# Feed-forwards with the gate and up weights as the stationary operand

## The chip, the cores and the metric

The kernel runs on one core of one Trainium2 chip. The metric is device time in microseconds for one execution, as the median of several runs. TensorE does the matrix products, VectorE and ScalarE the elementwise work, GpSimd (POOL) a few small steps; SyncE (SP) issues the transfers that bring the weights from HBM.

## What is computed

Three layers of a small model for 256 tokens with 1024 features, everything in float32. A first block (attention and gated convolution, modulated by rows computed from `c`) is followed by two more: gated linear attention, then differential attention. Each of the three ends in a gated feed-forward of 2816 hidden columns. The reference, cut to what the change concerns:

```python
def swiglu(h, w_gate, w_up, w_down):
    return (jax.nn.silu(h @ w_gate) * (h @ w_up)) @ w_down

# first block: one layer
x  = layer_norm(DEEPNORM_ALPHA * x + g1[:, None, :] * mix, ln1_g[l], ln1_b[l])
ff = swiglu(modulate(x, sh2, sc2), w_gate[l], w_up[l], w_down[l])
x  = layer_norm(DEEPNORM_ALPHA * x + g2[:, None, :] * ff, ln2_g[l], ln2_b[l])

# second block: two layers
def swiglu_2(h, w_in, w_out):
    g, u = split_cols(h @ w_in, [D_FF_2, D_FF_2])
    return (jax.nn.silu(g) * u) @ w_out

h = h + mix
h = h + swiglu_2(rms_norm(h, norm_ffn[i]), ffn_w_in[i], ffn_w_out[i])
gate = jax.nn.sigmoid(rms_norm(h, ple_norm[i]) @ ple_w_gate[i])
h = h + gate * (p[i] @ ple_w_proj[i])
```

## The kernel before

**Tiles.** The 256 tokens are two token tiles of 128, `x[0]` and `x[1]`, with tokens on the partitions and 1024 features along the free dimension. A product over the features needs them on the partitions, so each token tile is transposed on TensorE in blocks of 128x128 (`tr`, line 124, against the identity) and evacuated into tiles `xh` and `xl` of the class `XT` (L164). Every operand is split into two parts whose sum is the float32 value, `h` (a cast) and `l` (the rest, a subtraction). A product then is three matmuls: h by h, h by l, l by h (`mm3`, L157: lines L159, L160, L162). Of an `XT`, tile `[t][n]` holds four of the eight feature blocks for one token tile.

**Weights.** They are streamed once. `stage` (L127) issues the transfers, `gran` (L141) splits a granule of 128x1024 into `wh` (ScalarE's cast, L150) and `wl` (VectorE's subtraction, L151). Staging has eight buffers, the split weights five.

**The feed-forward** (`ffn`, L684) runs over eleven chunks of 256 hidden columns; there are three feed-forwards, so 33 chunks. Of a chunk, each granule holds two feature blocks by 512 columns: 256 of gate, 256 of up. The stationary operand of a matmul is a block of tokens (128 features x 128 tokens), the moving one 512 weight columns, and the result `ps[t]` holds tokens on the partitions, gate in the first 256 columns, up in the others: 8 feature blocks x 2 token tiles x 3 parts = 48 matmuls of 512 columns. ScalarE takes Silu of the gate half (L714, or L717 with the token's factor as `scale`), VectorE multiplies by the up half (L715, L718). The product `sg` has tokens on the partitions, and the down projection needs hidden columns there, so four transposes (L720, recorded at L124) put it into a PSUM bank, from which `hh` and `hl` are split (L723, L724). The down projection of the chunk before, 24 matmuls of 512 columns into four accumulating banks, stands behind the gate and up matmuls of the present one. The last two chunks are multiplied at the end, a token tile and a bank at a time (`finish`, L232).

**The factor r.** The second and third feed-forward (in `tail_layer`) stand behind an RMS norm whose factor per token, `rs[t]`, is one number per partition and is applied after the matmuls, to gate and up. `rms_of` (L741) computes it beside the first chunk. In the first feed-forward there is no such factor (`rs` is None); its input comes from `norm_pair` (L655), which normalizes token tile 0, then token tile 1: a residual and its sums (L662, L663), a mean and variance, the normalization (L674), transposes, an affine step per block (L191), a cast (L177) and a subtraction (L178). In the other two, `residual_rms` (L733) adds the residual (L736), transposes and evacuates with a gain (`put_gain`, L184 and L185).

**Order.** A scheduler sets the order on each engine from the program's order, dependences and buffers; it interleaves the transposes of a token tile with matmuls that are ready. PSUM has eight banks, four for `mm()` and four for `ac()`; the four accumulators of the down projection are the latter, so gate/up products and the transposed product share four.

The columns of the granule, as the gate/up matmuls read them:

```python
wh, wl = gran(stage(gu(g, c)), (2, 512))
for t in range(2):
    for i in range(2):
        kb = g * 2 + i
        xh, xl = xt(kb, t)
        mm3([ps[t]], xh, xl, [wh[:, i]], [wl[:, i]], kb == 0, kb == KB - 1)
```

## Time and profile before

| what | value |
|---|---|
| median of 3 runs | 1100.68 us (1100.53 to 1101.87) |
| span of the profiled execution | 1096.2 us |
| TensorE matmuls busy | 1028.7 us (94%), 4770 instructions |
| TensorE weight loads busy | 819.9 us (75%) |
| VectorE busy | 669.1 us (61%) |
| ScalarE busy | 569.7 us (52%) |
| HBM read | 192.60 MB, 177 GB/s over the span |

The span is the time between the first and last recorded instruction of one profiled execution; the runs are timed without the profiler. PE stands for TensorE's matmuls (transposes among them), PEld for its weight loads, DVE for VectorE, ACT for ScalarE. Matmuls are pipelined, so their recorded lengths overlap, and what a matmul takes in a stream is the distance from its start to the next one's. PEclk is the granted clock, 1.00 or 0.50 (2.4 or 1.2 GHz) of TensorE.

### The profile page before, as it was taken

Reading aid. Unit: us, or ns where it says so; the run is one execution under the profiler, and the core shown is the slowest. Engines: PE = TensorE matmul, PEld = TensorE weight load, DVE = VectorE, ACT = ScalarE, POOL = GpSimd, SP = SyncE. Lnnn points to the kernel's source line nnn. Section 1 sums busy time; section 2 is a strip of 40 time slices with the busy share of each in tenths; the row PEclk is TensorE's granted clock in tenths of the full one; section 3 lists DMA queues with packets and bytes.
Section 4 is the critical chain, followed back from the end, with each engine's and each line's share of the span. In section 5 each row is a group of like instructions: output and inputs, shape, how many; then the busy total and the mean of one; then the engine's idle time right before and its main releaser. Section 6 shows DMA issues by size and latency. Waiting matters only on the chain.

```text
span 1096.2 us, 13449 instructions
## 1 busy us (share of the span) xinstructions
PE 1028.7 (94%) x4770; PEld 819.9 (75%) x4770; DVE 669.1 (61%) x1037; ACT 569.7 (52%) x910; POOL 105.4 (10%) x76
## 2 busy tenths in 40 slices
PE   2888998899999989999999999998998999999998
PEld 1664767678888867888788888886776778888886
DVE  3775568645555654764755556577877675545644
ACT  2354546645545466654644445466656464444543
POOL 0011150302200040000000000004011000000000
PEclk9888899899999999999999999999999999999999
DMA  8864558467866606444665667543442366666711
GB/s 281 283 224 154 191 202 298 145 210 231 258 189 193 206 12 187 160 133 155 192 190 178 190 192 234 170 154 118 154 141 92 95 193 191 184 186 189 240 66 39
DMA packets 130864, 194.53 MB, mean 177 GB/s; under 512 B 10447, under 2 KB 92867, under 8 KB 130797
## 3 DMA queue, kind: packets, MB, share of 16 engines
q1 hardware_dynamic: 130584, 193.48, 55.8%
q8 instruction: 37, 0.61, 0.2%
q10 hardware_dynamic: 212, 0.20, 0.1%
q14 instruction: 31, 0.25, 0.1%
HBM read 192.60 MB, written 1.05 MB: 177 GB/s over the span
## 4 chain that ended last, share of the span: by engine, by line
PE 78%; DVE 10%; ACT 4%; DMA 2%; POOL 2%; issue 2%; SPq 1%; DVEq 0%; ACTq 0%; POOLq 0%
PE mmb L162 16%; PE mmb L160 15%; PE mmb L159 15%; PE acb L159 7%; PE acb L160 7%; PE acb L162 7%; PE acb L124 2%; POOL rs L265 2%; PE mmb L124 2%; DVE wl L151 2%; DMA st<-in_w_ada_dram 1%; ACT wh L150 1%; DVE part L333 1%; DVE xl L178 1%; PE acb L1054 1%
## 5 line engine op out<-in xcount | busy, mean ns | idle before, releaser
L151 DVE TENSOR_TENSOR wl<-st,wh 128x1024 fp32r<-128x1024 f32 (+4 forms) x292 | 357.2, 1228 | 243.6 <-ACT wh L150 240.1
L150 ACT CAST wh<-st 128x1024 fp32r<-128x1024 f32 (+4 forms) x292 | 301.3, 1038 | 262.0 <-PE mmb L162 162.4
L159 PE MATMUL mmb<-wh,xh 128*128 128x512 f32 (+4 forms) x904 | 358.8, 399 | 6.8 <-ACT wh L150 3.5
L162 PE MATMUL mmb<-wh,xl 128*128 128x512 f32 (+4 forms) x904 | 352.0, 394 | 7.3 <-DVE xl L178 7.0
L160 PE MATMUL mmb<-wl,xh 128*128 128x512 f32 (+4 forms) x904 | 355.4, 394 | 0.9 <-DVE wl L151 0.7
L162 PEld LDWEIGHTS mmb<-wh,xl 128*128 128x128 f32 x904 | 173.0, 191 | 45.6 <-DVE xl L178 9.4
L159 PEld LDWEIGHTS mmb<-wh,xh 128*128 128x128 f32 x904 | 172.8, 192 | 43.2 <-ACT xh L177 4.3
L160 PEld LDWEIGHTS mmb<-wl,xh 128*128 128x128 f32 x904 | 173.5, 192 | 35.5 <-DVE wl L151 3.0
L160 PE MATMUL acb<-wl,hh 128*128 128x512 f32 x216 | 85.3, 395 | 0.0
L159 PE MATMUL acb<-wh,hh 128*128 128x512 f32 x216 | 84.8, 393 | 0.0
L162 PE MATMUL acb<-wh,hl 128*128 128x512 f32 x216 | 67.2, 392 | 0.0
L747 POOL TENSOR_TENSOR rsx<-rsx,mhalf 128x1 f32<-128x1 f32 x12 | 10.3, 856 | 460.1 <-DVE rsx L746 460.1
L265 POOL TENSOR_TENSOR rs<-rs,mhalf 128x8 f32<-128x8 f32 (+1 forms) x18 | 32.7, 1820 | 207.7 <-DVE rs L264 175.1
L159 PEld LDWEIGHTS acb<-wh,hh 128*128 128x128 f32 x216 | 40.5, 188 | 10.3 <-ACT wh L150 0.8
L160 PEld LDWEIGHTS acb<-wl,hh 128*128 128x128 f32 x216 | 40.6, 188 | 9.1 <-issue 0.5
L162 PEld LDWEIGHTS acb<-wh,hl 128*128 128x128 f32 x216 | 40.6, 188 | 8.6
L338 POOL TENSOR_TENSOR part<-st,part 128x512 f32<-128x512 f32 x21 | 32.1, 1530 | 7.5 <-issue 6.0
L717 ACT ACTIVATE sg<-mmb,rsx 128x256 f32<-128x256 f32 x44 | 20.8, 474 | 22.9 <-PE mmb L162 20.8
L151 DVE TENSOR_TENSOR wxl<-st,wxh 128x1024 fp32r<-128x1024 f32 x22 | 26.8, 1221 | 5.2 <-ACT wxh L150 5.0
L150 ACT CAST wxh<-st 128x1024 fp32r<-128x1024 f32 x22 | 22.7, 1050 | 9.7 <-DMA st<-in_ffn_w_out_dram 4.8
L718 DVE SCALAR_TENSOR_TENSOR sg<-mmb,rsx,sg 128x256 f32<-128x256 f32 x44 | 20.9, 480 | 10.8 <-ACT sg L717 10.8
L184 ACT ACTIVATE xh<-acb,cols 128x128 fp32r<-128x128 f32 x64 | 20.7, 367 | 8.9 <-PE acb L124 6.1
(307 smaller groups left out, 1110.0 us busy)
## 6 DMA issues: line engine op xcount, KB each, us to landing
st<-in_ffn_w_in_dram SPq DMA_DIRECT2D x176, 256.0 KB
st<-in_ffn_w_out_dram SPq DMA_DIRECT2D x44, 512.0 KB
st<-in_w_ada_dram SPq DMA_DIRECT2D x32, 512.0 KB
st<-in_diff_w_in_dram SPq DMA_DIRECT2D x24, 512.0 KB
st<-in_w_gate_dram SPq DMA_DIRECT2D x44, 256.0 KB
st<-in_w_up_dram SPq DMA_DIRECT2D x44, 256.0 KB
st<-in_w_down_dram SPq DMA_DIRECT2D x22, 512.0 KB
st<-in_w_ada_dram SPq DMA_DIRECT2D x32, 256.0 KB
```

What stands on the lines that cost most here:

```text
L124: T.transpose(o, i, ident)
L150: A.copy(h[:, :n], src)
L151: V.tensor_sub(l[:, :n], src, h[:, :n].bitcast(F32))
L159: T.matmul(p_, xh, wh, start=start, stop=False)
L160: T.matmul(p_, xh, wl, start=False, stop=False)
L162: T.matmul(p_, xl, wh, start=False, stop=stop)
L178: V.tensor_sub(l, v, h.bitcast(F32))
L184: A.activation(h[:, i, :], b, AF.Copy, scale=g)
L265: G.tensor_tensor(r[:, :n], r[:, :n], mhalf[:, :n], op=OP.pow)
L338: G.tensor_add(part, w(kb), bias if kb == 0 else part)
L717: A.activation(sg, ps[t][:, 0:256], AF.Silu, scale=rs[t])
L718: V.scalar_tensor_tensor(sg, ps[t][:, 256:512], rs[t], sg, op0=OP.mult, op1=OP.mult)
```

## The change

In the feed-forwards the operands of the gate and up matmuls change places. The stationary operand is now a block of the weights (128 features x 128 hidden columns), the moving one a feature block of all 256 tokens (`xt.tokens(kb)`). The result has hidden columns on the partitions and tokens along the free dimension, as the down projection wants it; `ps[0]` holds the gate product of two column blocks, `ps[1]` the up product. A chunk has 8 feature blocks x 4 column blocks x 3 parts = 96 matmuls of 256 columns instead of 48 of 512. The four transposes of the product and its PSUM bank go; Silu, the product, `hh` and `hl` are each one operation on 512 columns, from `sg` in SBUF.

The token's factor r now runs along the free dimension. `across` spreads it: two diagonal matrices (identity times r), two matmuls with a matrix of ones into a PSUM bank, a copy to `rw`. Gate is multiplied by `rw` on VectorE before Silu; the factor of up is applied to the output of the down projection, in `residual_rms`. The `XT` tiles hold both token tiles (three tiles of twice the size for six). Other products read the same blocks as before.

```diff
-    xtp = ctx.enter_context(tc.tile_pool(name="xtp", bufs=6))
+    xtp = ctx.enter_context(tc.tile_pool(name="xtp", bufs=3))
...
-            self.h[t][n] = xtp.tile([P, 4, P], F32R, name="xh", tag="xh")
-            self.l[t][n] = xtp.tile([P, 4, P], F32R, name="xl", tag="xl")
...
+                self.h[n] = xtp.tile([P, 4, S], F32R, name="xh", tag="xh")
+                self.l[n] = xtp.tile([P, 4, S], F32R, name="xl", tag="xl")
...
+        def tokens(self, kb):
+            n, i = divmod(kb, 4)
+            return self.h[n][:, i, :], self.l[n][:, i, :]
...
+        def across(r):
+            rb = mm()
+            for t in range(2):
+                dg = sm.tile([P, P], F32, name="dg", tag="dg", bufs=2)
+                V.tensor_scalar(dg, ident, r[t], None, op0=OP.mult)
+                T.matmul(rb[:, t * P:(t + 1) * P], onesP, dg, start=t == 0, stop=t == 1)
+            rw = wk.tile([P, S], F32, name="rw", bufs=1)
+            A.copy(rw, rb[:, 0:S])
+            return rw
...
-                for t in range(2):
-                    for i in range(2):
-                        kb = g * 2 + i
-                        xh, xl = xt(kb, t)
-                        mm3([ps[t]], xh, xl, [wh[:, i]], [wl[:, i]], kb == 0, kb == KB - 1)
+                for i in range(2):
+                    kb = g * 2 + i
+                    xh, xl = xt.tokens(kb)
+                    for u in range(2):
+                        for j in range(2):
+                            o = ps[u][:, j * S:(j + 1) * S]
+                            ws = slice(u * 256 + j * P, u * 256 + j * P + P)
+                            T.matmul(o, wh[:, i, ws], xh, start=kb == 0 and j == 0, stop=False)
+                            T.matmul(o, wl[:, i, ws], xh, start=False, stop=False)
+                            T.matmul(o, wh[:, i, ws], xl, start=False, stop=kb == KB - 1 and j == 1)
+            if c == 0 and rs is not None:
+                rw = across(rs)
...
-            tp = mm()
-            tv = tp.rearrange("p (a b) -> p a b", b=S)
-            for t in range(2):
-                sg = wk.tile([P, 256], F32, name="sg", tag="sg", bufs=3)
-                if rs is None:
-                    A.activation(sg, ps[t][:, 0:256], AF.Silu)
-                    V.tensor_mul(sg, ps[t][:, 256:512], sg)
-                else:
-                    A.activation(sg, ps[t][:, 0:256], AF.Silu, scale=rs[t])
-                    V.scalar_tensor_tensor(sg, ps[t][:, 256:512], rs[t], sg, op0=OP.mult, op1=OP.mult)
-                for i in range(2):
-                    tr(tv[:, i, t * P:(t + 1) * P], sg[:, i * P:(i + 1) * P])
+            sg = wk.tile([P, 2, S], F32, name="sg", tag="sg", bufs=2)
+            gv, uv = v3(ps[0], S), v3(ps[1], S)
+            if rw is None:
+                A.activation(sg, gv, AF.Silu)
+            else:
+                V.tensor_tensor(sg, gv, rw[:, None, :].to_broadcast([P, 2, S]), op=OP.mult)
+                A.activation(sg, sg, AF.Silu)
+            V.tensor_mul(sg, uv, sg)
...
-            A.copy(hh, tv)
-            V.tensor_sub(hl, tv, hh.bitcast(F32))
+            A.copy(hh, sg)
+            V.tensor_sub(hl, sg, hh.bitcast(F32))
...
-            V.tensor_add(x[t][:, hs], src[t][n], x[t][:, hs])
+            if r is None:
+                V.tensor_add(x[t][:, hs], src[t][n], x[t][:, hs])
+            else:
+                V.scalar_tensor_tensor(x[t][:, hs], src[t][n], r[t], x[t][:, hs], op0=OP.mult, op1=OP.add)
```

Three places show what moves. On TensorE, at the start of the first feed-forward, the order before is this (`acb` is a PSUM bank that takes transposes of `x0` or `x1`, `mmb` a product, `ident` the identity; the transposes of `x0` stand further up, and behind them fifteen matmuls of token tile 0):

```order
L162 MATMUL mmb_1614<-wh_1638,xl_1542 128x512
L159 MATMUL mmb_1614<-wh_1657,xh_1556 128x512
L160 MATMUL mmb_1614<-wl_1658,xh_1556 128x512
L162 MATMUL mmb_1614<-wh_1657,xl_1557 128x512
L124 MATMUL acb_1576<-ident_82,x1_88 128x128 x4
L159 MATMUL mmb_1614<-wh_1657,xh_1556 128x512
L124 MATMUL acb_1591<-ident_82,x1_88 128x128 x4
L160 MATMUL mmb_1614<-wl_1658,xh_1556 128x512
L162 MATMUL mmb_1614<-wh_1657,xl_1557 128x512
```

and after, from the transposes of `x0` on:

```order
L126 MATMUL acb_1525<-ident_82,x0_89 128x128 x4
L126 MATMUL acb_1540<-ident_82,x0_89 128x128 x4
L126 MATMUL acb_1570<-ident_82,x1_90 128x128 x4
L126 MATMUL acb_1583<-ident_82,x1_90 128x128 x4
L728 MATMUL mmb_1604<-xh_1535,wh_1609 128x256
L729 MATMUL mmb_1604<-xh_1535,wl_1610 128x256
L728 MATMUL mmb_1605<-xh_1535,wh_1609 128x256
L729 MATMUL mmb_1605<-xh_1535,wl_1610 128x256
L728 MATMUL mmb_1741<-xh_1535,wh_1746 128x256
L729 MATMUL mmb_1741<-xh_1535,wl_1747 128x256
L730 MATMUL mmb_1604<-xl_1536,wh_1609 128x256
```

All four sets of transposes now stand ahead of the first gate/up matmul; before, those of `x1` stood in the midst of token tile 0's matmuls.

On ScalarE, at the end of chunk 0 of the second feed-forward, before (`L150` is the cast of a weight granule, `L184` a token block, `L717` Silu, `L723` the cast of the product):

```order
L184 ACTIVATE xh_4300<-acb_4295,cols_85 128x128 x2
L150 CAST wh_4460<-st_4457 128x1024
L184 ACTIVATE xh_4300<-acb_4295,cols_85 128x128
L150 CAST wh_4479<-st_4476 128x1024
L717 ACTIVATE sg_4403<-mmb_4324,rsx_4312 128x256
L717 ACTIVATE sg_4408<-mmb_4325,rsx_4317 128x256
L150 CAST wh_4497<-st_4495 128x1024
L723 CAST hh_4413<-mmb_4402 128x512
L150 CAST wh_4515<-st_4513 128x1024
```

and after (here the weight cast has line 152, Silu 746, the cast of the product 750; `rw` is the spread factor):

```order
L195 ACTIVATE xh_4690<-acb_4715,cols_85 128x128 x2
L152 CAST wh_4952<-st_4949 128x1024
L152 CAST wh_4983<-st_4980 128x1024
L152 CAST wh_5013<-st_5011 128x1024
L712 COPY rw_4875<-mmb_4868 128x256
L746 ACTIVATE sg_4877<-sg_4877 128x512
L152 CAST wh_5031<-st_5029 128x1024
L750 CAST hh_4881<-sg_4877 128x512
L152 CAST wh_5060<-st_5057 128x1024
```

The two Silu of 256 columns became one of 512, and a copy of `rw` stands ahead of it, behind a weight cast.

On TensorE, where the first feed-forward's last chunk ends, before (`acb_1610` and `acb_1611` are accumulators of the down projection, `hh_2919` the hidden tile of the last chunk but one, `hh_3012` that of the last):

```order
L162 MATMUL mmb_2924<-wh_2985,xl_1602 128x512
L124 MATMUL mmb_3001<-ident_82,sg_3002 128x128 x2
L159 MATMUL acb_1610<-wxh_3018,hh_2919 128x512
L160 MATMUL acb_1610<-wxl_3019,hh_2919 128x512
L162 MATMUL acb_1610<-wxh_3018,hl_2920 128x512
L159 MATMUL acb_1610<-wxh_3024,hh_2919 128x512
L124 MATMUL mmb_3001<-ident_82,sg_3007 128x128 x2
L160 MATMUL acb_1610<-wxl_3025,hh_2919 128x512
L162 MATMUL acb_1610<-wxh_3024,hl_2920 128x512
L159 MATMUL acb_1611<-wxh_3018,hh_2919 128x512
L160 MATMUL acb_1611<-wxl_3019,hh_2919 128x512
L159 MATMUL acb_1610<-wxh_3030,hh_3012 128x512
```

and after (`hh_3309` and `hh_3442` are those two tiles):

```order
L728 MATMUL mmb_3314<-xh_1550,wh_3411 128x256
L729 MATMUL mmb_3314<-xh_1550,wl_3412 128x256
L730 MATMUL mmb_3314<-xl_1551,wh_3411 128x256
L161 MATMUL acb_1600<-wxh_3448,hh_3309 128x512
L162 MATMUL acb_1600<-wxl_3449,hh_3309 128x512
L164 MATMUL acb_1600<-wxh_3448,hl_3310 128x512
L161 MATMUL acb_1600<-wxh_3454,hh_3309 128x512
L162 MATMUL acb_1600<-wxl_3455,hh_3309 128x512
L164 MATMUL acb_1600<-wxh_3454,hl_3310 128x512
L161 MATMUL acb_1601<-wxh_3448,hh_3309 128x512
L161 MATMUL acb_1600<-wxh_3460,hh_3442 128x512
L162 MATMUL acb_1600<-wxl_3461,hh_3442 128x512
```

The transposes of the product are gone; between the last gate/up matmul and the first that needs the last hidden tile stand seven matmuls.

## Rows read from the trace of the kernel before

**Rows 1.** Page: busy time, share, instructions; chain of waits by engine.
```profile
PE 1028.7 (94%) x4770; PEld 819.9 (75%) x4770; DVE 669.1 (61%) x1037; ACT 569.7 (52%) x910; POOL 105.4 (10%) x76
...
PE 78%; DVE 10%; ACT 4%; DMA 2%; POOL 2%; issue 2%; SPq 1%; DVEq 0%; ACTq 0%; POOLq 0%
```

**Rows 2.** By stretch: busy us of PE, PEld, DVE, ACT, POOL; PEclk, DMA, GB/s.
```profile
192.00:202.00 10.00, 6.79 (x15) 4.85 (x16) 5.17 (x7) 4.85 (x10) 4.30 (x3) 0.50 0.18 54
...
212.00:368.00 156.00, 156.00 (x710) 126.56 (x708) 87.80 (x89) 77.58 (x98) 13.93 (x8) 1.00 0.72 228
...
905.00:1045.00 140.00, 140.00 (x634) 115.41 (x633) 77.38 (x78) 66.82 (x79) 0.00 (x0) 1.00 0.64 201
...
430.80:434.80 4.00, 4.00 (x36) 4.00 (x35) 0.53 (x2) 3.97 (x4) 0.00 (x0) 1.00 0.41 132
```

**Rows 3.** PE timeline, one chunk: start, length, engine, line, instruction, count.
```profile
603.91 0.60 PE L124 MATMUL mmb<-ident,sg 128*128 128x128 f32 x4
...
604.58 0.39 PE L160 MATMUL mmb<-wl,xh 128*128 128x512 f32 x1
...
615.26 0.39 PE L159 MATMUL acb<-wh,hh 128*128 128x512 f32 x1
...
620.76 0.60 PE L124 MATMUL mmb<-ident,sg 128*128 128x128 f32 x4
```

**Rows 4.** Timeline of PE, the 256-column projection of the linear attention, at its end.
```profile
430.81 0.28 PE L159 MATMUL mmb<-wh,xh 128*128 128x256 f32 x1
...
434.77 0.40 PE L159 MATMUL mmb<-wh,xh 128*128 128x512 f32 x1
```

**Rows 5.** Instruction groups by form: busy us, mean ns; idle before, releaser.
```profile
L150 ACT CAST wh<-st 128x1024 fp32r<-128x1024 f32 x276 | 288.9, 1051 | 258.5 <-PE mmb L162 160.7 <-PE acb L162 84.7 <-issue 5.6
...
L124 PE MATMUL mmb<-ident,sg 128*128 128x128 f32 x132 | 21.1, 275 | 1.2 <-DVE sg L718 1.1
...
L723 ACT CAST hh<-mmb 128x512 fp32r<-128x512 f32 x33 | 19.2, 582 | 2.9 <-PE mmb L124 2.8
...
L663 DVE SCALAR_TENSOR_TENSOR x<-x,y 128x512 f32<-128x512 f32 x8 | 5.5, 691 | 0.2
...
L736 DVE TENSOR_TENSOR x<-mmb,x 128x512 f32<-128x512 f32 x8 | 5.5, 687 | 3.1 <-PE mmb L162 3.0
...
L929 ACT ACTIVATE sr<-mmb,rsx 128x512 f32<-128x512 f32 x4 | 2.6, 687 | 1.0 <-PE mmb L162 1.0
```

**Rows 6.** Timeline where the first feed-forward starts.
```profile
197.36 1.52 ACT L674 ACTIVATE x<-x,mu 128x512 f32<-128x512 f32 x2 [1.65 <-DVE mu L671]
...
202.75 1.86 ACT L191 ACTIVATE hT<-acb,m 128x128 f32<-128x128 f32 x5 [3.86 <-PE acb L124]
...
205.14 1.33 DVE L178 TENSOR_TENSOR xl<-hT,xh 128x512 fp32r<-128x512 f32 x1 [7.27 <-ACT xh L177]
...
206.85 2.43 DVE L178 TENSOR_TENSOR xl<-hT,xh 128x512 fp32r<-128x512 f32 x1 [0.38 <-ACT xh L177]
...
211.75 0.38 PE L124 MATMUL mmb<-ident,sg 128*128 128x128 f32 x2
```

**Rows 7.** Timeline where the second starts, and the end of its chunk 0.
```profile
525.80 2.38 DVE L185 SCALAR_TENSOR_TENSOR xl<-acb,cols,xh 128x128 fp32r<-128x128 f32 x8
...
535.90 0.39 PE L162 MATMUL mmb<-wh,xl 128*128 128x512 f32 x1
...
536.41 0.44 PE L124 MATMUL mmb<-ident,sg 128*128 128x128 f32 x2
```

**Rows 8.** Timeline where the third starts, and the end of its chunk 0.
```profile
880.37 0.60 DVE L185 SCALAR_TENSOR_TENSOR xl<-acb,cols,xh 128x128 fp32r<-128x128 f32 x2
...
889.51 1.28 ACT L717 ACT_TABLE_LOAD   x1 [0.30 <-PE mmb L162]
...
890.40 0.39 PE L162 MATMUL mmb<-wh,xl 128*128 128x512 f32 x1
...
891.86 0.44 PE L124 MATMUL mmb<-ident,sg 128*128 128x128 f32 x2 [1.07 <-DVE sg L718]
```

More of the change, by code (lines that the diff above doesn't have):

```diff
@@ L121, in body @@
     G.memset(mhalf, -0.5)
+    onesP = const.tile([P, P], F32, name="onesP")
+    G.memset(onesP, 1.0)
     def tr(o, i):
@@ L165, in __init__, with new, part @@
         def __init__(self):
-            self.h = [[None, None], [None, None]]
-            self.l = [[None, None], [None, None]]
-        def new(self, t, n):
-            self.h[t][n] = xtp.tile([P, 4, P], F32R, name="xh", tag="xh")
-            self.l[t][n] = xtp.tile([P, 4, P], F32R, name="xl", tag="xl")
-            return self.h[t][n], self.l[t][n]
+            self.h = [None, None]
+            self.l = [None, None]
+        def new(self, n):
+            if self.h[n] is None:
+                self.h[n] = xtp.tile([P, 4, S], F32R, name="xh", tag="xh")
+                self.l[n] = xtp.tile([P, 4, S], F32R, name="xl", tag="xl")
+        def part(self, t, n):
+            self.new(n)
+            return self.h[n][:, :, t * P:(t + 1) * P], self.l[n][:, :, t * P:(t + 1) * P]
+        def tokens(self, kb):
+            n, i = divmod(kb, 4)
+            return self.h[n][:, i, :], self.l[n][:, i, :]
         def put(self, t, n, ps):
-            h, l = self.new(t, n)
+            h, l = self.part(t, n)
             v = ps.rearrange("p (a b) -> p a b", b=P)
@@ L180, in put_gain @@
         def put_gain(self, t, n, ps, gain):
-            h, l = self.new(t, n)
+            h, l = self.part(t, n)
             for i in range(4):
@@ L196, in __call__ @@
             n, i = divmod(kb, 4)
-            return self.h[t][n][:, i, :], self.l[t][n][:, i, :]
+            ts = slice(t * P, (t + 1) * P)
+            return self.h[n][:, i, ts], self.l[n][:, i, ts]
     def blocks_t(src, bank):
@@ L366, in block1 @@
             for n in range(2):
-                for t in range(2):
-                    xt.new(t, n)
+                xt.new(n)
             def qcols(q):
@@ L392, in quarter @@
                     for t in range(2):
-                        h, l = (a[t][q // 2][:, q % 2 * 2:q % 2 * 2 + 2, :] for a in (xt.h, xt.l))
+                        h, l = (a[:, q % 2 * 2:q % 2 * 2 + 2, :] for a in xt.part(t, q // 2))
                         src = v3(hT[:, t * 256:t * 256 + 256], P)
@@ L691, in hid @@
             return lambda t: (hh[:, i, t * P:(t + 1) * P], hl[:, i, t * P:(t + 1) * P])
+        def across(r):
[7 more added lines that the diff above has]
+            return rw
+        rw = None
         for c in range(NCH):
@@ L731, in ffn, with residual_rms @@
         return acc
-    def residual_rms(t, src, gain, xt, bank):
+    def residual_rms(t, src, gain, xt, bank, r=None):
         for n in range(2):
             hs = slice(n * 512, n * 512 + 512)
-            V.tensor_add(x[t][:, hs], src[t][n], x[t][:, hs])
+            if r is None:
+                V.tensor_add(x[t][:, hs], src[t][n], x[t][:, hs])
+            else:
+                V.scalar_tensor_tensor(x[t][:, hs], src[t][n], r[t], x[t][:, hs], op0=OP.mult, op1=OP.add)
             xt.put_gain(t, n, blocks_t(x[t][:, hs], bank), gain)
@@ L958, in tail_layer @@
             for t in range(2):
-                residual_rms(t, acc, PLEG[i], hx, mm)
+                residual_rms(t, acc, PLEG[i], hx, mm, rs)
             rs = [rms_of(t, junk) for t in range(2)]
```

1 line of the change is left out of this document (removed).

## The prediction, made before the changed kernel ran

> **What bounds the kernel now.** I read the busy times and the chain of waits first: TensorE is busy for 94% of the span and carries 78% of the chain that ends last [rows 1]. Then I cut out the steady part of the feed-forwards, the loops over eleven chunks of 256 hidden columns that the change rewrites: in the two stretches shown TensorE is busy for every microsecond, at the full granted clock, while VectorE and ScalarE work for about half of it [rows 2]. So inside the loops only the time between TensorE's instructions counts. Their records cannot be read as lengths (a 512-column matmul is recorded longer than the distance to the next one and overlaps it); I read starts. Last I looked at where each feed-forward begins and ends, because the new form needs its inputs in another order [rows 6 to 8].
>
> **Steady chunks: what goes.** From one set of transposes (L124, 603.91) to the next (620.76) is one chunk: 16.85 us [rows 3]. The second gate/up matmul starts at 604.58 and the first of the down projection at 615.26, 47 matmuls later: 10.68/47 = 0.2272 us each. The four transposes and the matmul behind them take 604.58 - 603.91 = 0.67; less one matmul, the transposes cost 0.44 us a chunk. The rest is the down projection, which stays.
>
> A record of these transposes has 275 ns [rows 5], but four of them take 0.44 us of the path, so they are pipelined like matmuls and their records overlap. The Trainium skill, "TensorE: Matmul & The Clock Gate", section "Part 4: PE-mode transpose", gives about 275 ns for a transpose in a kernel. Taken as a price on the path, the 132 that go would be worth 36 us instead of 15, and the kernel would come out near 1092; the starts in rows 3 speak against it.
>
> **What comes.** 96 matmuls with 256 moving columns take the place of 48 with 512. The kernel already has that shape in one projection (128x256, the same split products): 33 matmuls from 430.81 to 434.77 take 3.96 us, 0.1200 each [rows 4], with TensorE full [rows 2]. Half of 0.2272 would be 0.1136, so a pair of halves costs 12.8 ns more than the whole. Chunk after: 16.85 - 0.44 - 48 x 0.2272 + 96 x 0.1200 = 17.02, that is +0.17; times 33 chunks **+5.6 us**. (The halves alone cost 33 x 0.61 = +20.3, the transposes give back 14.6.) Each nanosecond of spacing is worth 3168 x 1 ns = 3.2 us, so this is the term to be careful with. I take 0.1200, since it is the same shape in a stream without gaps, with 0.1195 to 0.1225 as bounds: 1.6 us less to 7.9 us more. The upper bound is there because the weight loads fill that stretch (4.00 of 4.00 us) where they take four fifths of the 512-column ones [rows 2], and because that stream lasts 48 matmuls and no longer.
>
> **VectorE and ScalarE in a chunk.** Silu, product, cast and subtraction become one operation each on 512 columns. By rows of that width these are about 0.69 (L929), 0.69 (L736), 0.58 (L723) and 0.69 us [rows 5]; the second and third feed-forward add a product by r, 0.69. The hidden tile is used one chunk later, behind 96 matmuls of 0.12, so 11.5 us cover a chain of under 4, and both engines keep idle time [rows 2]. Cost 0; what it costs without the cover is the end terms below. At the residual L736 becomes the form of L663, 687 against 691 ns [rows 5]: 0.
>
> **Start of the first feed-forward.** Before, token tile 0's matmuls run while tile 1 is still being normalized, at half the clock (0.50 granted from 192 to 202) [rows 2]. After, the first matmul needs both tiles. Tile 1's normalization starts at 197.36 and takes 1.52, to 198.9; its transposes no longer stand behind matmuls, so the affine steps (1.86 for five, so 1.5 for four) end at 200.4, the cast (0.58) at 201.0, the subtraction (1.33) at 202.4 [rows 5, 6]. The third matmul waits for that. Then 94 matmuls x 0.12 = 11.3. TensorE has little to do before, so I charge the first 17 of them at the half level, 0.213 instead of 0.12: +1.6 (bounds 0 and 2.3). Chunk 0 then ends at 215.3 against 211.75; less the 0.61 that the sum above already has for it, **+2.9 us**. If the subtraction takes 2.43, as the next one there does [rows 6], 1.1 more; if the matmuls start at full clock, 1.6 less.
>
> **Start of the second.** Before, chunk 0 ends at 535.45, two matmuls of chunk 1 ahead of 535.90, and the transposes come at 536.41, 0.28 later than the spacing asks [rows 7]. After, the third matmul needs the correction of tile 1's first block. VectorE makes these from 525.80, eight in 2.38 us; the third of them is ready at 526.7 [rows 7]. 526.7 + 11.3 = 538.0: +2.55 - 0.61 - 0.28 = **+1.7**. **Third:** the wanted one is ready at 880.97 [rows 8], so chunk 0 ends at 892.3 against 889.95, two matmuls ahead of 890.40; and the stall before the transposes (890.40 to 891.86, where 0.23 would do, behind a table load of 1.28 on ScalarE) goes, as nothing on TensorE waits for that product any more: +2.35 - 0.61 - 1.23 = **+0.5**. Bounds of each: 1.5 less if other matmuls fill the wait, 1.6 more if the pause drops the clock for the first 17 matmuls.
>
> **r along the free dimension.** In the second and third, VectorE scales the identity by r (two of 128x128, about 0.3 each by L185 [rows 7]), two small matmuls spread it and ScalarE copies it. This borrows a PSUM bank while chunk 0 still holds two and chunk 1 asks for two; there are four. The order shows ten matmuls (1.2 us) between the second small one and the first that needs the bank back, and on ScalarE a weight cast (1.05 [rows 5]) ahead of the copy. I charge **+0.5** each, bounds 0 and 1.1.
>
> **Ends.** The last hidden tile is wanted soon after its last gate/up matmul: the order puts 7 matmuls (1.6 us) between in the first, 17 (3.9) in the second, 10 (2.3) in the third. The chain Silu, product, cast is 0.69 + 0.69 + 0.58 = 1.96 [rows 5], with hand-overs some 2.4; with the product by r 3.1. Before, it ran in halves, the first one early. **+0.8, 0, +0.8**; bounds 0, and 1.05 more where a weight cast stands ahead on ScalarE.
>
> **Sum:** 5.6 + 2.9 + 1.7 + 0.5 + 2 x 0.5 + 1.6 = +13.3 on the profiled 1096.2, a span of 1109.5. The median of the runs is 1100.68, 4.5 us over the span: **1114 us**.
>
> **Rivals.** *Halves cost half* (faster): if a 256-column matmul took 0.1136 us in the new stream, the steady term would be -14.6, and the time 1100.7 - 14.6 + 7.7 = 1094. It decides below 0.1158 (13.3/3168 = 4.2 ns less). Against it is the row of 33 [rows 4]; for it only that weights, not activations, are loaded here. Chance 0.04. The Trainium skill, same page, section "Back-to-back issue gap", has N/2.4 + 2.5 ns for a single matmul, so 109.2 and 215.8; a pair of halves would cost 2.5 ns more than the whole and the time would be 1098. Both rows lie 11 ns above that formula, and no row here shows so small a gap. *The edges are hidden*: starts and ends cost nothing, as matmuls of chunk 1 fill the waits; 1106. For it is that the order draws some of them forward; against it, that these need both tiles too. Chance 0.15. *The stream does not hold 0.120*: the loads leave no slack, 0.124 gives 12.7 more, 1127. Against it is that 0.1200 is exact over the whole row. Chance 0.12. *The change does not do what it says*: the order shows 96 matmuls a chunk and no transposes of the product; 0.01. What is left, 0.68, is the forecast, 1109 to 1118.
>
> **Numbers.** About 2.2 us (0.2%) can be told from no change here. Faster by more: 0.04. Within: 0.04, a smaller spacing together with hidden edges. Slower: 0.92. The range runs from hidden edges to a spacing of 0.1225: 1105.5 to 1122.
>
> **What would show it.** Right: 17.0 us between equal matmuls of neighbouring chunks, starts 0.120 apart, no idle TensorE inside the loops; chunk 0 of the first feed-forward ending 3 to 4 us later; TensorE idle about 0.5 us for the copy of r. Wrong: a spacing under 0.116 or over 0.1225; a granted clock below 1.00 within the loops; TensorE waiting for a weight cast or subtraction in mid-loop.

## The result, and the profile after

| | before | after |
|---|---|---|
| median of 4 runs each | 1100.61 us (1097.38 to 1101.87) | 1112.62 us (1111.32 to 1114.94) |
| span of the profiled execution | 1096.2 us | 1109.5 us |
| TensorE matmuls | 1028.7 us, 4770 | 1038.5 us, 6230 |
| TensorE weight loads | 819.9 us | 897.0 us |

The changed kernel takes 1.0114 times as long, with a 95% interval of 1.0092 to 1.0135: 12 us slower. The page of the profile after, part 1 and the chain of waits by engine, reads as before [rows 1], with a larger share for TensorE:

```profile
PE 1038.5 (94%) x6230; PEld 897.0 (81%) x6230; DVE 679.2 (61%) x1030; ACT 564.1 (51%) x879; POOL 105.3 (9%) x77
...
PE 79%; DVE 8%; ACT 4%; DMA 3%; POOL 2%; issue 2%; SPq 1%; ACTq 0%; POOLq 0%; DVEq 0%
```

The stretches of the first and second feed-forward (by stretch: busy us of PE, PEld, DVE, ACT, POOL; PEclk, DMA share, GB/s), each first from its start to the first down-projection matmul, then the loop; then the stretch between the second and the third, and the start of the third:

```profile
189.30:228.10 38.80, 28.72 (x211) 27.27 (x210) 23.09 (x22) 23.21 (x38) 11.16 (x5) 0.82 0.46 143
...
228.10:368.00 139.90, 139.90 (x983) 129.39 (x982) 77.26 (x69) 69.04 (x79) 14.28 (x8) 1.00 0.69 217
...
522.10:555.90 33.80, 31.91 (x234) 30.45 (x233) 21.79 (x37) 19.07 (x34) 2.07 (x2) 0.95 0.50 149
...
555.90:691.90 136.00, 136.00 (x962) 128.04 (x961) 76.80 (x76) 62.42 (x68) 0.00 (x0) 1.00 0.64 195
...
721.60:891.30 169.70, 156.50 (x750) 122.90 (x749) 128.44 (x272) 101.94 (x203) 27.18 (x16) 0.97 0.38 122
...
891.30:916.00 24.70, 24.52 (x199) 23.84 (x198) 17.19 (x28) 14.81 (x25) 1.49 (x1) 1.00 0.70 214
```

The loops are as full as they were [rows 2], but the weight loads now fill 92 and 94% of them (129.39 of 139.90, 128.04 of 136.00). The two starts run below the full clock (0.82, 0.95). In the last row but one TensorE does the work that it did before, in a stretch that the change leaves alone. One chunk in the loop, from one down-projection matmul to the next chunk's, with the first gate/up matmul between (start, length, engine, line, instruction):

```profile
606.89 0.40 PE L161 MATMUL acb<-wh,hh 128*128 128x512 f32 x1
...
612.41 0.28 PE L728 MATMUL mmb<-xh,wh 128*128 128x256 f32 x1
...
623.90 0.39 PE L161 MATMUL acb<-wh,hh 128*128 128x512 f32 x1
```

The chunk takes 623.90 - 606.89 = 17.01 us, where it took 16.85 [rows 3], and the 96 matmuls 623.90 - 612.41 = 11.49, 0.1197 each.

Taking the starts of the same instructions in both timelines, the two spans can be laid side by side. A start reaches from the normalization (first) or the sum of squares of a token tile (tile 0 in the second, tile 1 in the third) to the first down-projection matmul and holds two chunks of gate and up; a loop holds eight chunks; an end reaches to the next stage's work behind it (the first copy of the projection of `p` on ScalarE in the first, the first matmul of the embedding's gate in the others) and holds the last chunk. The forecast column is the prediction's terms put into the same stages, 0.17 a chunk included.

| stage | before, us | after, us | difference | forecast |
|---|---|---|---|---|
| ahead of the first feed-forward | 187.81 | 189.27 | +1.46 | 0 |
| first: start, loop, end | 35.35, 138.67, 32.90 | 38.84, 139.87, 32.54 | +3.49, +1.20, -0.36 | +3.2, +1.4, +1.0 |
| linear attention | 122.63 | 121.53 | -1.10 | 0 |
| second: start, loop, end | 30.50, 134.79, 30.12 | 33.80, 136.08, 29.70 | +3.30, +1.29, -0.42 | +2.5, +1.4, +0.2 |
| gate of the embedding, differential attention | 167.00 | 169.70 | +2.70 | 0 |
| third: start, loop, end | 23.52, 134.99, 30.15 | 24.66, 136.08, 29.85 | +1.14, +1.09, -0.30 | +1.3, +1.4, +1.0 |
| behind the third | 27.79 | 27.62 | -0.17 | 0 |
| sum | 1096.2 | 1109.5 | +13.3 | +13.3 |

The span came out as forecast to the tenth, and partly by luck: the ends went the other way (-1.1 instead of +2.1), and stages that the change doesn't touch hold +2.9.

### The profile page after: what moved, and what is told of

It is laid out like the page before. It is cut to its first block, busy times and chain, and to the rows that moved or that the text cites. A ratio compares the mean times of both kernels' runs of the same rounds, so it can differ in the third digit from the quotient of the medians.

```text
span 1109.5 us, 16400 instructions
## 1 busy us (share of the span) xinstructions
PE 1038.5 (94%) x6230; PEld 897.0 (81%) x6230; DVE 679.2 (61%) x1030; ACT 564.1 (51%) x879; POOL 105.3 (9%) x77
## 4 chain that ended last, share of the span: by engine, by line
PE 79%; DVE 8%; ACT 4%; DMA 3%; POOL 2%; issue 2%; SPq 1%; ACTq 0%; POOLq 0%; DVEq 0%
PE mmb L728 12%; PE mmb L730 12%; PE mmb L729 11%; PE acb L161 7%; PE acb L164 7%; PE acb L162 7%; PE mmb L164 5%; PE mmb L162 5%; PE mmb L161 5%; PE acb L126 2%; POOL rs L277 2%; DVE wl L153 2%; DMA st<-in_w_ada_dram 1%; ACT wh L152 1%; PE acb L1084 1%
## 5 line engine op out<-in xcount | busy, mean ns | idle before, releaser
L728 PE MATMUL mmb<-xh,wh 128*128 128x256 f32 x1056 | 301.0, 285 | 3.5 <-ACT xh L188 1.6
L729 PE MATMUL mmb<-xh,wl 128*128 128x256 f32 x1056 | 300.0, 284 | 0.0
L730 PE MATMUL mmb<-xl,wh 128*128 128x256 f32 x1056 | 299.1, 284 | 0.1
L728 PEld LDWEIGHTS mmb<-xh,wh 128*128 128x128 f32 x1056 | 202.5, 192 | 6.1 <-ACT xh L188 2.0
L729 PEld LDWEIGHTS mmb<-xh,wl 128*128 128x128 f32 x1056 | 202.4, 192 | 1.2
L730 PEld LDWEIGHTS mmb<-xl,wh 128*128 128x128 f32 x1056 | 201.8, 192 | 0.5 <-DVE xl L196 0.3
L161 PE MATMUL mmb<-wh,xh 128*128 128x512 f32 (+4 forms) x376 | 149.0, 401 | 4.2 <-ACT wh L152 3.5
L162 PE MATMUL mmb<-wl,xh 128*128 128x512 f32 (+4 forms) x376 | 149.5, 399 | 0.8 <-DVE wl L153 0.7
L164 PE MATMUL mmb<-wh,xl 128*128 128x512 f32 (+4 forms) x376 | 145.8, 398 | 3.3 <-DVE xl L189 3.3
L161 PEld LDWEIGHTS mmb<-wh,xh 128*128 128x128 f32 x376 | 73.1, 196 | 19.5 <-ACT wh L152 4.1
```

The source lines that it names most:

```text
L161: T.matmul(p_, xh, wh, start=start, stop=False)
L162: T.matmul(p_, xh, wl, start=False, stop=False)
L164: T.matmul(p_, xl, wh, start=False, stop=stop)
L728: T.matmul(o, wh[:, i, ws], xh, start=kb == 0 and j == 0, stop=False)
L729: T.matmul(o, wl[:, i, ws], xh, start=False, stop=False)
L730: T.matmul(o, wh[:, i, ws], xl, start=False, stop=kb == KB - 1 and j == 1)
```

## Experiments: the parts of a chunk

**Transposes alone.** The kernel before without the four transposes; the product goes to SBUF and is split from there:

```diff
-            tp = mm()
-            tv = tp.rearrange("p (a b) -> p a b", b=S)
+            tv = wk.tile([P, 2, S], F32, name="sg", tag="sg", bufs=2)
             for t in range(2):
-                sg = wk.tile([P, 256], F32, name="sg", tag="sg", bufs=3)
+                sg = tv[:, t, :]
...
-                for i in range(2):
-                    tr(tv[:, i, t * P:(t + 1) * P], sg[:, i * P:(i + 1) * P])
```

> The kernel before, with the four transposes of each chunk's product left out: the hidden tile is split straight from the product, so the down projection multiplies blocks that are not transposed (values are not those of the reference, the work is the same otherwise). My sum: 0.44 us a chunk on the path, 33 x 0.44 = 14.6 us less than before, 1086, chunk period 16.41. A price of 275 ns for each of the 132 transposes on the path would give 36 us less, 1064. If the transposes were hidden beside the matmuls: 1100 and a period of 16.85.

Measured: 1086.25 us against 1101.98, ratio 0.986 (0.9843 to 0.9876). Neighbouring down projections in its loop (PE timeline):

```profile
574.45 0.39 PE L159 MATMUL acb<-wh,hh 128*128 128x512 f32 x1
...
590.82 0.39 PE L159 MATMUL acb<-wh,hh 128*128 128x512 f32 x1
```

The period is 16.37 us, so four transposes cost 0.48 a chunk in the loops (11.65 us over the 24 chunks of the three loops), 0.04 more than I read, and 0.96, 0.91 and 0.96 at the ends. That is 0.12 us for a transpose. The about 275 ns that the Trainium skill gives for a transpose in one kernel ("TensorE: Matmul & The Clock Gate", section "Part 4: PE-mode transpose") are the length of a record here too [rows 5]; taken as a cost in a stream it would be more than twice what leaving them out gives back.

**Halves alone.** The kernel before with every gate/up matmul cut in two:

```diff
-                        mm3([ps[t]], xh, xl, [wh[:, i]], [wl[:, i]], kb == 0, kb == KB - 1)
+                        for j in range(2):
+                            js = slice(j * 256, j * 256 + 256)
+                            o = ps[t][:, js]
+                            T.matmul(o, xh, wh[:, i, js], start=kb == 0 and j == 0, stop=False)
+                            T.matmul(o, xh, wl[:, i, js], start=False, stop=False)
+                            T.matmul(o, xl, wh[:, i, js], start=False, stop=kb == KB - 1 and j == 1)
```

> The kernel before, with every 512-column matmul of gate and up issued as two of 256 columns (activations still stationary, transposes still there). My sum: 96 x 0.1200 instead of 48 x 0.2272, +0.61 us a chunk, +20.3 us, 1121, chunk period 17.46. If a pair of halves costs only 2.5 ns more than the whole: +4 us, 1105, period 16.97. If the spacing of 0.120 needs the weights to be the stationary operand, the period differs from 17.46 in either direction.

Measured: 1123.84 us (1118.68 to 1130.23), ratio 1.0201 (1.0148 to 1.0254). In its loop:

```profile
608.92 0.39 PE L159 MATMUL acb<-wh,hh 128*128 128x512 f32 x1
...
626.36 0.39 PE L159 MATMUL acb<-wh,hh 128*128 128x512 f32 x1
```

The period is 17.44, +0.59 where I had +0.61. So a pair of halves costs 12.3 ns more than the whole, with the activations as the stationary operand as well: it is the number of matmuls that costs, not which operand stands still. Every matmul here has its own weight load, so no run tells what of it is the load's. By the formula for a single matmul that the Trainium skill has ("TensorE: Matmul & The Clock Gate", section "Back-to-back issue gap"), a pair of halves would cost an estimated 2.5 ns more; this run has about five times that. The two experiments add up to most of the change in the loops (-0.48 + 0.59 = +0.11 against +0.16; the other 0.05 a chunk is not accounted for), and at the ends (-0.96 + 0.55 = -0.41, -0.91 + 0.57 = -0.34, -0.96 + 0.55 = -0.41, against -0.36, -0.42, -0.30).

## Experiments: the starts

**Chunk 0 in the old form.** The changed kernel, but the first chunk of each feed-forward with tokens stationary:

```diff
         for c in range(NCH):
+            if c == 0:
+                ps = [mm(), mm()]
+                for g in range(KB // 2):
+                    wh, wl = gran(stage(gu(g, c)), (2, 512))
+                    for t in range(2):
+                        for i in range(2):
+                            kb = g * 2 + i
+                            xh, xl = xt(kb, t)
+                            mm3([ps[t]], xh, xl, [wh[:, i]], [wl[:, i]], kb == 0, kb == KB - 1)
...
+                continue
```

> The changed kernel, with chunk 0 of each feed-forward in the old form (tokens stationary, 512 weight columns moving, four transposes of the product), so that the first matmuls need token tile 0 alone. If the starts cost what they do because both token tiles are waited for: the first feed-forward starts 3 us and the second 2.5 us faster, the third 0.5 us, each chunk 0 is 0.16 shorter, together 6 us less than the changed kernel, 1106 to 1107. If the starts are late for another reason (the spread of r, the clock alone), the time stays at 1112.

The starts became 36.14, 31.22 and 24.07 us: 2.70, 2.58 and 0.59 less than in the changed kernel, 5.9 together, as expected. The spread of r is still in this kernel, so it isn't what they came from. The time did not follow: median 1111.63, ratio 1.0058 (1.0023 to 1.0093), and its ten runs lie in two groups, four from 1098.9 to 1104.1 and six from 1111.5 to 1113.4. In the profiled run, of the second group, the gain went into the stretch between the second and third feed-forward, where no line differs: 175.40 us against 169.70 in the changed kernel. By stretch, this kernel there:

```profile
717.00:892.40 175.40, 162.91 (x753) 126.69 (x751) 128.71 (x272) 101.99 (x204) 27.17 (x16) 0.93 0.37 118
```

and the kernel before:

```profile
712.80:879.80 167.00, 154.04 (x753) 121.39 (x751) 127.98 (x271) 101.92 (x204) 27.14 (x16) 0.99 0.40 124
```

The same 753 matmuls, and VectorE and ScalarE with the same work (128.71 and 127.98, 101.99 and 101.92 us busy); what differs is PEclk, 0.93 against 0.99. (The expectations further down count this stretch from the first sum of squares behind the second feed-forward, which is 5.0 us more here, 180.4, and 6.2 more in the kernel before, 173.2.)

**The changed kernel again**, on the chip of these runs, to see which of the differences outside the feed-forwards repeat:

> The changed kernel again, beside the others on one chip. In its first trace the stretches outside the feed-forwards, which the change leaves alone, took 1.5 us more ahead of the first, 1.1 less between the first and second and 2.9 more between the second and third than in the trace of before. If these are differences between executions of the same work (where the clock is granted), they come out otherwise in these four traces; if they follow from the change, they stay.

1113.7 us, ratio 1.0108 (1.0084 to 1.0131). Its trace repeats the first to 0.04 us in every stage but the one ahead of the first feed-forward (188.68 instead of 189.27). So the expectation that chance alone would spread them was wrong for this kernel; whether they follow from the change, these two traces could not tell.

**The same kernel, other traces.** Nothing is edited here.

> The kernel with chunk 0 in the old form once more, for another trace: its ten timed runs fell into two groups, 1099 to 1104 and 1111 to 1113, and its trace (1111.8) is of the second. If the groups are the clock in the differential attention, every stage of the feed-forwards has the same length as in that trace to 0.1 us, and in a run of the first group the stretch between the second and third feed-forward is 6 to 10 us shorter than 175.4, at a higher granted clock. If the groups come from the feed-forwards, their stages differ.

> The same kernel a third time, in case the trace before is of the same group again: same expectation.

1100.04 and 1103.3 us. The loops of the three traces agree to 0.01 us, the second and third start and the ends to 0.03, the first start only to 1.02 (36.14, 35.98, 35.12), where 0.1 was expected. The stretch between the second and third took 165.66 and 167.02 us:

```profile
715.00:880.60 165.60, 152.32 (x751) 120.03 (x750) 128.14 (x272) 101.89 (x203) 27.17 (x16) 1.00 0.39 125
```

```profile
716.90:883.90 167.00, 155.50 (x752) 122.62 (x751) 128.25 (x272) 102.07 (x203) 27.17 (x16) 0.98 0.39 124
```

One kernel, and the same stretch takes 165.6 us at PEclk 1.00, 167.0 at 0.98 and 175.4 at 0.93. In the slowest of the three the half clock was granted in three spans:

```profile
788.30:798.50 10.20, 10.20 (x30) 7.11 (x29) 7.47 (x21) 5.28 (x19) 0.00 (x0) 0.50 0.18 52
836.10:839.50 3.40, 3.40 (x11) 2.52 (x9) 2.62 (x5) 1.53 (x3) 1.68 (x1) 0.50 0.05 11
853.10:863.40 10.30, 10.30 (x26) 6.45 (x26) 5.86 (x16) 4.71 (x13) 0.00 (x0) 0.50 0.16 53
```

Its matmuls come in the same order as in the fastest, and start by start the two traces stay within 0.3 us of each other up to 788.3. Then the slower one falls back by 4.4, 1.5 and 4.7 us inside these three spans; outside them it loses nothing and makes up 0.8. So the granted clock makes the difference of 9.7 us, which is most of the 11.7 between these two executions as a whole. A difference of 2.7 us in this stretch between two kernels is no effect of an edit by itself. The spread reaches further in the kernel cut in halves:

```profile
726.80:904.30 177.50, 164.65 (x753) 127.96 (x752) 128.38 (x271) 102.10 (x203) 27.17 (x16) 0.92 0.36 116
```

**Is it the pause?** In the differential attention TensorE waits 1.5 us for the first exponentials, and in several traces the half clock starts there. Two attempts to fill it; first with matmuls into a bank of their own:

```diff
                     e = heads(hp, t)
+                    if hp == 2 * n and t == 1:
+                        dm = mm()
+                        for _ in range(4):
+                            T.matmul(dm[:, 0:256], kT[:, 4 * n, 0:P], kT[:, 4 * n, :], start=True, stop=True)
```

> The kernel with chunk 0 in the old form, and four matmuls whose result nobody reads placed in each of the two pauses of 1.5 us of the differential attention, where TensorE waits for the first exponentials. In the trace of the kernel without them, the half clock is granted after these pauses and the stretch between the second and third feed-forward takes 180.4 us, against 173.2 and 174.7 in the two kernels compared. If those pauses cost the clock: the stretch falls to about 174 and the runs gather at 1099 to 1104 instead of 1099 to 1113. If the clock there is granted for other reasons: runs of both kinds as before, median 1111.

1132.4 us, ratio 1.0273 (1.0235 to 1.0311): it tells nothing on the question, because with the borrowed bank the scheduler took matmuls out of the stretch ahead of the pause. There TensorE now waited for VectorE between sets of transposes (idle before, and its releaser, in brackets):

```profile
769.42 0.66 PE L126 MATMUL acb<-ident,r 128*128 128x128 f32 x4 [2.01 <-DVE r L1095]
...
774.71 1.11 PE L126 MATMUL acb<-ident,r 128*128 128x128 f32 x4 [4.63 <-DVE r L1095]
...
779.31 1.12 PE L126 MATMUL acb<-ident,r 128*128 128x128 f32 x4 [3.49 <-DVE r L1095]
```

and the granted clock over that stretch was half:

```profile
772.00:786.00 14.00, 7.13 (x27) 5.22 (x28) 9.82 (x19) 2.98 (x10) 1.94 (x2) 0.51 0.38 112
```

Then with score matmuls issued twice, which needs no bank:

```diff
-                    T.matmul(b[:, i * S:(i + 1) * S], qT[s * 64:s * 64 + 64, 2 * hp + i, ts_],
-                             kT[s * 64:s * 64 + 64, 2 * hp + i, :], start=True, stop=True)
+                    for _ in range(2 if hp % 2 == 0 and t == 1 else 1):
+                        T.matmul(b[:, i * S:(i + 1) * S], qT[s * 64:s * 64 + 64, 2 * hp + i, ts_],
+                                 kT[s * 64:s * 64 + 64, 2 * hp + i, :], start=True, stop=True)
```

> The kernel with chunk 0 in the old form; in the differential attention the four score matmuls of the second token tile are issued twice each, the second time with the same result, in both halves (16 matmuls of 256 columns in all become 24 where TensorE waits for the first exponentials). The filled pause of the experiment before borrowed a bank, and the scheduler then moved the value projection out of the stretch, so it told nothing; this one needs no bank and moves less. If the pause of 1.5 us costs the clock there, the stretch between the second and third feed-forward falls from 180.4 to 174 and runs gather at 1100 to 1104. If not, the runs stay of two kinds, 1099 to 1113, or the stretch grows by the repeated work.

1111.84 us (1111.45 to 1112.47), ratio 1.0091 (1.0062 to 1.0121); all four runs are of the slower group.

```profile
717.50:891.30 173.80, 159.42 (x766) 125.10 (x765) 127.95 (x268) 101.00 (x200) 28.13 (x16) 0.96 0.38 119
```

The half clock came all the same, but this run doesn't answer the question either, since the pause was not filled. The repeated matmuls ran ahead of it, the scheduler moved others too, and TensorE still waited for the exponentials, longer than before (first this run, then the kernel without the repetition in its slowest and its fastest trace):

```profile
787.23 0.66 PE L126 MATMUL acb<-ident,e 128*128 128x128 f32 x2 [1.72 <-DVE e L1126]
```

```profile
787.10 0.41 PE L126 MATMUL acb<-ident,e 128*128 128x128 f32 x2 [1.53 <-DVE e L1125]
```

```profile
785.41 0.41 PE L126 MATMUL acb<-ident,e 128*128 128x128 f32 x2 [1.50 <-DVE e L1125]
```

The last two settle half of it: the same pause, 1.53 and 1.50 us, stands in the trace where the half clock follows and in the one with PEclk 1.00 throughout the stretch. The pause alone is not enough. What makes the chip grant less there in one execution and not in another stays open.

## Experiments: a version that beats both

The loops lose because the new form has twice the matmuls. High and low part of the activations meet the same block `wh`; side by side they make one moving operand of 512 columns, and 3 matmuls of 256 become one of 512 and one of 256. The product then has two halves that must be added.

```diff
-                    for u in range(2):
-                        for j in range(2):
-                            o = ps[u][:, j * S:(j + 1) * S]
...
+            for j in range(2):
+                pj = [mm(), mm()]
+                for kb in range(KB):
...
+                    xh, xb = xt.tokens(kb)
+                    for u in range(2):
+                        ws = slice(u * 256 + j * P, u * 256 + j * P + P)
+                        T.matmul(pj[u], wh[:, i, ws], xb, start=kb == 0, stop=False)
+                        T.matmul(pj[u][:, 0:S], wl[:, i, ws], xh, start=False, stop=kb == KB - 1)
...
+                    A.copy(o[:, j, :], ps[j][u][:, 0:S])
+                    V.tensor_add(o[:, j, :], ps[j][u][:, S:2 * S], o[:, j, :])
```

> The kernel with chunk 0 in the old form, and in the other 30 chunks one matmul of 512 columns for both parts of the activations (high and low side by side, one load of the weights' high part) and one of 256 for the low part of the weights, instead of three of 256; the two halves are added behind (a copy and an addition more for each of four blocks a chunk, on ScalarE and VectorE), a chunk is done in two passes. By the spacings: 32 x (0.2272 + 0.1200 - 0.3600) = -0.41 us a chunk, period 16.60, 30 x 0.41 = 12.3 us less than the kernel with chunk 0 in the old form: 1087 to 1100 by the clock in the differential attention. If the weights held over two passes make TensorE wait for buffers: a period over 17.0 and no gain.

1103.97 us, ratio 1.0025 (1.0007 to 1.0043). Loops 137.36, 133.57, 133.57: 2.5 us less than with three matmuls, 0.31 a chunk instead of 0.41. But the linear attention took 127.21 where it took 121.57: there the order of TensorE's instructions was another. The tile held the high and low part of each block in turn, and other readers of it were ordered differently. And the sums of squares behind the second and third end came 2.3 and 1.4 us later, which I took for the additions ahead of the last hidden tile. So the next version keeps the parts in separate halves of the tile and does the last chunk with three matmuls of 256:

```diff
-                b = xtp.tile([P, 4, 2, S], F32R, name="xb", tag="xb")
-                self.b[n], self.h[n], self.l[n] = b, b[:, :, 0, :], b[:, :, 1, :]
+                b = xtp.tile([P, 2, 4, S], F32R, name="xb", tag="xb")
+                self.b[n], self.h[n], self.l[n] = b, b[:, 0], b[:, 1]
...
+            last = c == NCH - 1
+            if last:
+                ps = [mm(), mm()]
```

> The kernel with the high and low part side by side (one 512-column matmul and one of 256 in place of three of 256), with two things mended that its trace showed: the two parts lie in halves of the tile that do not interleave, so that other readers' order is that of the kernel with chunk 0 in the old form again, and the last chunk is done with three matmuls of 256, so that no additions stand ahead of the last hidden tile. Against that kernel: 27 chunks x 0.32 = 8.6 us less in the loops, the stretch between the first and second feed-forward back from 127.2 to 121.6 us, the ends back from 25.1 and 27.0 to 23.7 and 24.7. Time 1092 where the clock in the differential attention is like that of the hi-lo run before (172.3), up to 1103 where it is not. If the additions or the buffers hold TensorE up elsewhere, 1100 or more in all runs.

1097.2 us in ten runs (1093.94 to 1104.03), before 1101.9 beside it: ratio 0.9965 (0.9942 to 0.9987), faster than before by some 4 us, and 15 less than the changed kernel's 1112.6 and 1113.7. Its page, part 1, and three down projections in a loop:

```profile
PE 1029.8 (94%) x5234; PEld 842.9 (77%) x5234; DVE 712.0 (65%) x1139; ACT 598.1 (55%) x990; POOL 103.4 (9%) x77
```

```profile
580.92 0.40 PE L161 MATMUL acb<-wh,hh 128*128 128x512 f32 x1
...
597.52 0.39 PE L161 MATMUL acb<-wh,hh 128*128 128x512 f32 x1
...
614.31 0.40 PE L161 MATMUL acb<-wh,hh 128*128 128x512 f32 x1
```

Periods of 16.60 and 16.79 take turns, where 16.60 was worked out; linear attention 122.81, third start 23.62, loops 137.18 and twice 133.57. Why every second chunk takes 0.19 more was not followed. The first mend worked: the linear attention has the order of the kernel with chunk 0 in the old form again, and most of the 1.2 us that it still takes more (122.81 against 121.57) comes with a second span at half clock (428.2 to 431.6). The second was not needed: by the first matmul of the next stage, the second and third end took 29.59 and 29.62 us before it and 29.74 and 29.81 with it. Counted by the stages of the feed-forwards alone, this kernel takes 586.4 us where the one before takes 591.0 (their starts, loops and ends added up), so the gain does not come from the clock elsewhere.

## Why the prediction was right, point by point

**The steady chunk** holds: +0.16 a chunk (17.01 against 16.85) where +0.17 was worked out, from 0.1197 us a matmul against 0.1200 read [rows 4]. Both parts were a little off and in the same sense: transposes 0.48 instead of 0.44, halves 0.59 instead of 0.61. The spacing seen for 48 matmuls holds for 96 in a row, with the loads filling 92 to 94% of the time; the rival of a stream that cannot hold it is out, and so is the one that halves cost half.

**The start of the first** was sized right: +3.49 with two chunks, against 3.2. These are the rows that the steps named, in the trace after (normalization, subtraction, first matmul, first that needs the subtraction):

```profile
198.83 1.52 ACT L685 ACTIVATE x<-x,mu 128x512 f32<-128x512 f32 x2 [1.65 <-DVE mu L682]
...
203.24 1.46 DVE L189 TENSOR_TENSOR xl<-hT,xh 128x512 fp32r<-128x512 f32 x1 [3.91 <-ACT xh L188]
...
203.26 0.58 PE L728 MATMUL mmb<-xh,wh 128*128 128x256 f32 x1 [1.60 <-ACT xh L188]
...
204.76 0.58 PE L730 MATMUL mmb<-xl,wh 128*128 128x256 f32 x1
```

From the normalization to the first matmul it is 4.43 us; 3.6 was worked out (197.36 to 201.0). The subtraction took 1.46 instead of 1.33, so the first matmul that needs it came 5.93 us after the normalization instead of 5.0. Two errors went the other way. That matmul is the seventh, as the order on record shows, and not the third as the steps had it, so four more ran in the wait. And only nine matmuls from it on went at half spacing (until 206.85), where seventeen were charged, a number that no row gave. The sum was nearly right because these errors cancel: chunk 0 ended 17.8 us after the normalization, 17.9 were worked out. That the start is long because both token tiles are waited for is borne out by the old form of chunk 0: 2.7 of 3.5 us come back (2.9 and 3.7 in its two later traces). The first feed-forward has no r to spread.

**The start of the second** was sized too small by 0.8: +3.30 against 2.5. The step that failed is the choice between its bounds: the clock. I took the full clock there and gave 1.6 us more as the bound for a drop; it dropped, after TensorE had waited 1.36 and 0.49 us (idle before and releaser in brackets):

```profile
529.79 0.39 PE L728 MATMUL mmb<-xh,wh 128*128 128x256 f32 x1 [1.36 <-ACT xh L195]
...
531.24 0.58 PE L728 MATMUL mmb<-xh,wh 128*128 128x256 f32 x1 [0.49 <-ACT wh L152]
```

From there starts are 0.21 us apart until 534.6, and PEclk of the stretch is 0.95. Fifteen matmuls at 0.21 instead of 0.12 are 1.4 us, more than the 0.8 that was missing; a part of it was made up because five gate/up matmuls instead of two ran ahead of the first that needs a correction (531.62), the rest was not worked out. In the third feed-forward it did not drop (PEclk 1.00 in the row of its start, 891.30 to 916.00): +1.14 against 1.3.

**The spread of r** waits as described, for the copy behind a weight cast, but for less, and its own matmuls cost something too. On ScalarE and TensorE in the third:

```profile
904.10 0.39 PE L710 MATMUL mmb<-dg,onesP 128*128 128x128 f32 x2
...
904.24 0.36 PE L729 MATMUL mmb<-xh,wl 128*128 128x256 f32 x1
...
904.34 1.05 ACT L152 CAST wh<-st 128x1024 fp32r<-128x1024 f32 x1 [1.83 <-PE mmb L730]
...
904.44 0.28 PE L730 MATMUL mmb<-xl,wh 128*128 128x256 f32 x1
...
905.30 0.36 ACT L712 COPY rw<-mmb 128x256 f32<-128x256 f32 x1
...
905.40 0.28 PE L729 MATMUL mmb<-xh,wl 128*128 128x256 f32 x1
...
905.71 0.39 PE L728 MATMUL mmb<-xh,wh 128*128 128x256 f32 x1
```

The last two matmuls start 0.31 us apart instead of 0.12, so the wait is 0.19 and not 0.5. Cast and copy are behind each other as the order said: the copy starts 0.96 after the cast and takes 0.36, 1.32 us against ten matmuls of 0.12. The small matmul of the second token tile (L710, two records) was charged nothing; from 904.10 to 904.44 two gate/up starts would take 0.12 each and it adds some 0.2 (0.34 - 0.12 = 0.22). Together that is 0.4, near the 0.5 charged, with the share of the wait too large.

**The ends** are the step that was wrong: forecast +0.8, 0, +0.8 beside the chunk's 0.17, measured -0.36, -0.42, -0.30. The first end, in the trace after (Silu, last gate/up matmul, product, cast, first use of the last hidden tile as the second of two):

```profile
384.48 0.60 ACT L743 ACTIVATE sg<-mmb 128x512 f32<-128x512 f32 x1 [1.27 <-PE mmb L730]
...
384.88 0.28 PE L730 MATMUL mmb<-xl,wh 128*128 128x256 f32 x1
...
385.27 0.69 DVE L747 TENSOR_TENSOR sg<-mmb,sg 128x512 f32<-128x512 f32 x1 [1.01 <-PE mmb L730]
...
385.99 0.62 ACT L750 CAST hh<-sg 128x512 fp32r<-128x512 f32 x1
...
386.39 0.78 PE L161 MATMUL acb<-wxh,hh 128*128 128x512 f32 x2
```

I let Silu, product and cast, 2.4 us, begin at the last gate/up matmul. But gate's columns are complete before up's: Silu starts at 384.48, 0.4 us before the last matmul does, and only product and cast are left behind it, 385.27 to 386.61. Seven matmuls from 385.00 on, 0.23 us apart, cover that but for some hundredths. And I charged the old form too little: its transposes come there in two pairs, and by the run without them they cost 0.96 at an end, twice what they cost in the loop.

**Outside the feed-forwards** the forecast was 0 and the trace says +2.9. This is the granted clock. In these stretches TensorE's instructions have the same order before and after, and start by start the traces part where one of them has the half clock and the other has not. In the differential attention all of the +2.7 comes in this span of the trace after, which the one before ran at full clock:

```profile
794.00:800.80 6.80, 6.80 (x21) 4.79 (x20) 5.21 (x15) 4.14 (x16) 0.00 (x0) 0.50 0.26 78
```

In the linear attention each had one such span, at another place, after and before:

```profile
408.30:411.70 3.40, 3.40 (x12) 3.27 (x11) 2.71 (x3) 3.05 (x6) 1.18 (x1) 0.50 0.02 5
```

```profile
413.70:417.10 3.40, 3.40 (x12) 3.31 (x12) 1.60 (x4) 2.97 (x6) 0.55 (x1) 0.50 0.77 232
```

The forecast hit the span because an error of -3.2 in the ends met this +2.9 and the +0.8 of the second start. Counted by the feed-forwards alone, the change costs 10.4 us (+7.9 in starts, +3.6 in loops, -1.1 at ends), in two traces that agree to 0.04 us a stage.

**The chances.** Slower by over 0.2% had 0.92, and was right. *Hidden edges* (0.15) is out: the starts cost 7.9 of the 10.4 us, and 5.9 of them come back when chunk 0 needs one token tile at a time (1.4 of these by the clock, which then doesn't fall in the second).

## What to carry to other kernels

Count matmuls, not columns: in a stream where each has its own weight load, two of 256 columns cost 12 ns more than one of 512 here, so swapping the operands pays only if the transposes that it saves (0.12 us each) outweigh the matmuls that it adds, or if two moving operands for the same weights are put side by side to get the width back. An operand that spans all tokens makes the first matmul wait for the last token tile; the first chunk can keep the old form. And compare stages, not spans, where an untouched stretch can move by as much as the effect; laying two traces side by side start by start shows where they part.

## What was unexpected of the hardware

With the same instructions the differential attention and the gate ahead of it took 165.7, 167.0 and 175.4 us in three executions of one kernel, and up to 177.5 in another kernel, at granted clocks of 1.00, 0.98, 0.93 and 0.92, and between the first and the third of these the time was lost inside spans at the half clock alone. For each kernel the runs lean to one side: the kernel before stayed between 1097.7 and 1104.0 in the runs beside these experiments but for 1107.0 and 1105.4, the changed one between 1110.8 and 1117.1. And matmuls of 256 columns, each with its own weight load, ran 96 in a row at 0.1197 us.
